# Attention with folded blocks: the own block's scores copied over the preceding block's, two transpositions a unit, and a ring of five buffers for the parted weights

## The chip, the cores and the metric

The kernel runs on one core of a Trainium2 chip. The metric is the device time of one execution in microseconds; the time before is the median of three runs. The profile shows one further execution, recorded by the hardware profiler. Engines are named as in the profile: PE is TensorE's matmul, PEld its weight load, DVE is VectorE, ACT is ScalarE, POOL is GpSimd, SP is SyncE.

## What is computed

Four layers with residual connections over 1040 tokens (16 learned ones ahead of a sequence of 1024), width 1024, in fp32. Layers 0 and 3 are sliding-window attention, layer 1 is an mLSTM, layer 2 an HGRN2. Only the attention is touched (and one small helper in layer 2). Its core, cut to what matters:

```
qb, kb, vb: blocks of 128 tokens; 16 query heads, 4 key heads, width 64
kk = concatenate([prev(kb), kb]); vv = concatenate([prev(vb), vb])
s = einsum('bnqhgd,bnkhd->bnhgqk', qb, kk) * (A_HD ** -0.5)
dist = (arange(BLOCK)[:, None] + BLOCK) - arange(2 * BLOCK)[None, :]
mask = (dist >= 0) & (dist < A_WIN)          # A_WIN = 128 = BLOCK
m = maximum(s.max(axis=-1), sink)
e = exp(where(mask, s, -inf) - m)
p = e / (e.sum(axis=-1) + exp(sink - m))
o = einsum('bnhgqk,bnkhd->bnqhgd', p, vv)
```

A query at place i of its block sees the keys j > i of the preceding block and the keys j <= i of its own: exactly 128 of the 256, one for each j.

## The kernel before, in words

Activations lie transposed (features on partitions, tokens along the free axis) in three chunks of 400, 384 and 256 tokens. Each projection is done with operands parted into a high and a low half of type fp32r: a copy rounds to the high half, a subtraction gives the low half, and three products (high by high, high by low, low by high) replace one. Weights are loaded and parted by `weights` and `split` (copy on ACT, L195, subtraction on DVE, L196); the projections' matmuls are at L231 and L326.

PE's instructions are issued in the order of one long list of steps. Each step is a cost in ns, a function that issues the instructions, and perhaps a function that prepares weights, which is called ahead by a sum of costs (`LOOKAHEAD`). `weave` interleaves two lists in proportion to their costs; `later`, `spread` and `chain` place steps behind others. The orders on DVE, ACT and POOL are left to the framework's planner; `hi` raises a step's priority there. Each engine works off its queue in order.

The attention's core is cut into units: one block of queries, one of the four pairs of query tiles (`ts`, index u) and one half `hh`, so two heads a unit. Layer 0 has 4 x 9 x 2 = 72 units, the last layer, which leaves out block 0, has 64. A unit goes through three steps, and in the list the k-th S step stands behind the T step of unit k - 2 (`T_LAG`) and the V step of unit k - 4 (`V_LAG`), woven with projections.

- `S_step`: scores of two heads against up to 256 keys in one PSUM tile (L726, L727). DVE's tensor_tensor_reduce adds the mask, scales by the query's norm, writes the negated scores to the tile `Sm` and their minimum to `st` (L734). ACT takes the exponential with the sum (L737). POOL, which has put the sinks in the column behind the scores (L731), multiplies by DVE's reciprocal of the sum (L739, L740).
- `T_step`: the weights are transposed into the PSUM tile `pt`, one 128x128 piece for each of two key blocks and two heads, so four (L755). ACT rounds to `Ph` (L757), DVE subtracts for `Pl` (L758).
- `V_step`: value products with `Ph` and `Pl` for each key block (L773); at the end of a group of blocks the result goes out by L781 and L782.

For block 0 there is one key block of 16 tokens, for block 1 one of 16 and one of 128, for the others two of 128. The masks tile holds a 128x128 part for sums over heads and, from column 128, the values 0 inside the band and 1e30 outside it. `Ph`, `Pl` and `Sm` have two buffers each. In layer 0 the second query projection borrows them as temporaries (`idle`).

Of the kernel before, what the change touches and what calls it, by code (L numbers as in the profile page):

```python
# [113 lines left out]
def hybrid_kernel(ctx: ExitStack, tc: tile.TileContext, ins, out, layers=(0, 1, 2, 3)):  # L114
# [29 lines left out]
    def small(w):  # L144
        return tpool.tile([P, w], F32, tag=f"s{w}", name=nm("s"), bufs=12 if w < 8 else 4)

# [333 lines left out]
    def layer_a(i, j, first, last, fin, scale=None):  # L480
# [4 lines left out]
        def enter():  # L485
            R["mix"] = mix = new_mix()
            R["masks"] = masks = mix.tile([P, 384], F32, name=nm("masks"))
            sp.dma_start(masks, ins["a_masks"])
            R["cons"] = cons = mix.tile([P, 18], F32, name=nm("cons"))
            sp.dma_start(cons, ins["a_cols"][j])  # L490
            v.tensor_scalar(cons[:, 0:1], cons[:, 0:1], -0.125, None, op0=ALU.mult)
            v.tensor_scalar(cons[:, 2:18], cons[:, 2:18], -1.0, None, op0=ALU.mult)
# [57 lines left out]
        def idle(n, c0, cn):  # L550
            z = [R["mix"].tile([P, 2, 2, P], F32, tag=z, name=nm(z), bufs=2) for z in ("Ph", "Pl")]
            z = [y.rearrange("p a u q -> p (a u q)") for y in z]
            z.append(R["mix"].tile([P, 2, 257], F32, tag="Sm", name=nm("Sm"), bufs=2).rearrange("p u k -> p (u k)"))
            return [y[:, :cn] for y in z]
# [143 lines left out]
        def mixers():  # L698


            def S_step(w):
# [12 lines left out]
                w["kbs"] = kbs  # L714
                nk = sum(z[2] for z in kbs)
                kw, mo = (nk if b == 0 else 256), {0: 128, 1: 112}.get(b, 0)
                kb = slice(k0, k0 + kw)
                S = psum("pm", 2).rearrange("p (u k) -> p u k", u=2)
                w["Sm"] = Sm = mix.tile([P, 2, 257], F32, tag="Sm", name=nm("Sm"), bufs=2)
                if b == 0:  # L720
# [3 lines left out]
                for u, t in enumerate(w["ts"]):  # L724
# [5 lines left out]
                    if u == 0:  # L730
                        g.tensor_copy(Sm[:nq, :, nk : nk + 1], cons[:nq, 2 + head : 4 + head].rearrange("p (u c) -> p u c", c=1))  # L731
                for u in range(2):
                    rq = R["rq", w["ts"][u], n][:nq, 2 * kq + hh : 2 * kq + hh + 1]
                    v.tensor_tensor_reduce(Sm[:nq, u, :nk], S[:nq, u, :nk], R["masks"][:nq, P + mo : P + mo + nk],  # L734
                                           rq, sinks[u], ALU.add, ALU.min, st[:nq, u : u + 1])
# [7 lines left out]
            def T_step(w):  # L743
                b, kbs, Sm = w["b"], w["kbs"], w["Sm"]
                nq = blk(b)[1]
                kn = NMETA if b == 0 else P
                pt = psum("pt", 1).rearrange("p (k u q) -> p k u q", k=2, u=2)
                w["Ph"] = Ph = R["mix"].tile([P, 2, 2, P], F32R, tag="Ph", name=nm("Ph"), bufs=2)
                w["Pl"] = Pl = R["mix"].tile([P, 2, 2, P], F32R, tag="Pl", name=nm("Pl"), bufs=2)
                if b == 0:  # L750
                    for z in (Ph, Pl):
                        g.memset(z[:, 0, :, :NMETA].bitcast(F32), 0.0)
                for ki, (kb, ko, _) in enumerate(kbs):
                    for u in range(2):
                        pe.transpose(pt[:kn, ki, u, :], Sm[:, u, ko : ko + kn], ident)  # L755
# [386 lines left out]
    def layer_c(i, j, fin):  # L1142
# [3 lines left out]
        def enter():  # L1146
# [9 lines left out]
            def lse(dst, p0, p1):  # L1156
                d = small(8)
                v.tensor_tensor(d, p0, p1, op=ALU.subtract)
# [397 lines left out]
def _layout(inp):  # L1556
# [3 lines left out]
    f["ngain"] = np.asarray(inp["norm_gain"]).reshape(4, KT, P).transpose(2, 0, 1)  # L1560
    am = np.zeros((P, 384), np.float32)
    am[:64, :64] = 1.0
    am[64:, 64:128] = 1.0
    ii = np.arange(P)[:, None]
    jj = np.arange(256)[None]
    am[:, 128:] = np.where((jj > ii) & (jj <= ii + P), 0.0, -BIG)
# [78 lines left out]
```

## Time and profile before

| what | value |
|---|---|
| median of 3 runs | 2595.16 us (2594.36 to 2595.36) |
| profiled execution, its own time | 2594.76 us |
| profiled execution, span from first to last instruction | 2593.0 us |
| mean granted TensorE clock | 0.997 |
| instructions | 54342 |
| POOL busy | 243.4 us |

The span leaves out what lies ahead of the first and behind the last instruction, here 1.8 us. Busy times are the shares in which an engine worked on at least one instruction. Matmuls are pipelined, so the duration of one includes time in which the next runs already; what one matmul costs is read from start to start. The two attention layers lie at about 0 to 460 us and 2140 to 2593 us.

### The profile page before, as it was taken

What the parts mean: (1) busy time and instruction counts of PE and PEld (TensorE: products, weight loads), DVE (VectorE), ACT (ScalarE), POOL (GpSimd) and SP (SyncE); (2) the same over time, 40 slices, a digit from 0 to 9 for tenths busy, and PEclk for the clock granted to TensorE, in tenths of its full rate; (3) what the DMA queues carried; (4) which work ended last, traced back from release to release, by engine and by line L of the source; (5) the groups of instructions that cost most, each with busy time, mean ns of one, the idle gap of its engine ahead of it and who ended that gap; (6) DMA issues with size and microseconds to landing.
All of it is one profiled execution on the core that took longest, in us unless ns stands there. A gap on an engine that the chain in (4) does not pass through costs nothing.

```text
span 2593.0 us, 54342 instructions
## 1 busy us (share of the span) xinstructions
PE 2547.2 (98%) x20446; PEld 2487.2 (96%) x20446; DVE 1949.5 (75%) x5266; ACT 1682.9 (65%) x4403; POOL 243.4 (9%) x564
## 2 busy tenths in 40 slices
PE   8999999999999999999999999999999999999999
PEld 8899999999999999999999999999999999999999
DVE  7897898785657474747475688978878978887996
ACT  8766766576464555555555757877676857767772
POOL 0321231000000000000000000001000000321330
PEclk9999999999999999999999999999999999999999
DMA  5223212021111111111111111111111113212112
GB/s 157 62 66 95 57 43 70 29 67 54 46 50 49 51 41 58 42 50 45 53 42 50 58 35 34 35 35 35 34 42 34 35 51 93 64 43 82 56 42 78
DMA packets 86058, 140.21 MB, mean 54 GB/s; under 512 B 12425, under 2 KB 39186, under 8 KB 85794
## 3 DMA queue, kind: packets, MB, share of 16 engines
q1 hardware_dynamic: 85794, 136.73, 17.1%
q8 instruction: 161, 2.64, 0.4%
q14 instruction: 103, 0.84, 0.1%
HBM read 121.83 MB, written 4.27 MB: 49 GB/s over the span
## 4 chain that ended last, share of the span: by engine, by line
PE 62%; DVE 13%; ACT 8%; issue 2%; DMA 1%; SPq 0%; POOL 0%; DVEq 0%; ACTq 0%; POOLq 0%
PE pj L231 28%; PE pj L326 14%; PE pj L281 10%; DVE wl L196 1%; PE po L1019 1%; PE po L1021 1%; PE pa L1035 1%; ACT X L1269 1%; PE po L773 1%; DVE x L329 1%; PE pj L277 1%; ACT Sm L737 1%; PE pt L755 1%; DVE Sm L734 1%; DVE X L1267 1%
## 5 line engine op out<-in xcount | busy, mean ns | idle before, releaser
L231 PE MATMUL pj<-uh,wh 128*128 128x256 f32 (+2 forms) x2688 | 915.7, 341 | 7.7 <-ACT uh L401 7.2
L231 PE MATMUL pj<-ul,wh 128*128 128x256 f32 (+2 forms) x2688 | 864.3, 322 | 0.3
L231 PE MATMUL pj<-uh,wl 128*128 128x256 f32 (+2 forms) x2688 | 864.6, 322 | 0.0
L231 PEld LDWEIGHTS pj<-uh,wh 128*128 128x128 f32 x2688 | 508.5, 189 | 17.4 <-ACT uh L401 7.2
L231 PEld LDWEIGHTS pj<-ul,wh 128*128 128x128 f32 x2688 | 508.8, 189 | 6.4 <-DVE ul L196 0.8
L231 PEld LDWEIGHTS pj<-uh,wl 128*128 128x128 f32 x2688 | 507.9, 189 | 0.0
L196 DVE TENSOR_TENSOR wl<-wr,wh 128x512 fp32r<-128x512 f32 (+1 forms) x338 | 234.2, 703 | 55.0 <-ACT wh L195 52.1
L195 ACT CAST wh<-wr 128x512 fp32r<-128x512 f32 (+1 forms) x338 | 202.7, 613 | 97.6 <-PE pj L326 31.5
L326 PE MATMUL pj<-yh,wh 128*128 128x384 f32 (+2 forms) x768 | 253.6, 330 | 9.8 <-DVE x L329 8.3
L329 DVE TENSOR_TENSOR x<-x,pj 128x384 f32<-128x384 f32 (+2 forms) x480 | 233.8, 507 | 33.4 <-PE pj L326 32.1
L326 PE MATMUL pj<-yh,wl 128*128 128x384 f32 (+2 forms) x768 | 246.2, 321 | 0.0
L326 PE MATMUL pj<-yl,wh 128*128 128x384 f32 (+2 forms) x768 | 246.2, 321 | 0.0
L281 PE MATMUL pj<-wh,uh 128*128 128x256 f32 (+1 forms) x768 | 232.7, 303 | 0.0
L281 PE MATMUL pj<-wl,uh 128*128 128x256 f32 (+1 forms) x768 | 216.3, 282 | 0.0
L281 PE MATMUL pj<-wh,ul 128*128 128x256 f32 (+1 forms) x768 | 215.9, 281 | 0.0
L737 ACT ACTIVATE Sm<-Sm,s 128x257 f32<-128x257 f32 (+2 forms) x272 | 131.1, 483 | 88.6 <-DVE s L734 86.3
L740 POOL TENSOR_TENSOR Sm<-Sm,s 128x512 f32<-128x512 f32 (+2 forms) x136 | 139.3, 1024 | 406.5 <-DVE s L739 386.3
L458 ACT ACTIVATE t<-t 128x384 f32<-128x384 f32 (+2 forms) x240 | 118.0, 491 | 75.5 <-DVE t L457 74.6
L195 ACT CAST yh<-r 128x384 fp32r<-128x384 f32 (+2 forms) x120 | 57.0, 478 | 156.2 <-PE pj L326 139.4
L326 PEld LDWEIGHTS pj<-yh,wh 128*128 128x128 f32 x768 | 144.9, 189 | 14.0 <-DVE x L329 10.3
L457 DVE SCALAR_TENSOR_TENSOR t<-pj,t 128x400 f32<-128x400 f32 (+2 forms) x168 | 86.3, 513 | 81.5 <-ACT t L456 80.2
L281 PEld LDWEIGHTS pj<-wh,uh 128*128 128x128 f32 x768 | 144.7, 188 | 2.2
(303 smaller groups left out, 5447.1 us busy)
## 6 DMA issues: line engine op xcount, KB each, us to landing
wr<-in_b_win SPq DMA_DIRECT2D x124, 256.0 KB, 2.8
wr<-in_a_win SPq DMA_DIRECT2D x80, 256.0 KB, 2.8
wr<-in_c_win SPq DMA_DIRECT2D x64, 256.0 KB, 3.0
wr<-in_a_wout SPq DMA_DIRECT2D x32, 256.0 KB, 2.8
wr<-in_b_wout SPq DMA_DIRECT2D x32, 256.0 KB, 2.7
t<-t SPq DMA_DIRECT2D x100, 48.0 KB, 1.9
cs<-in_rope SPq DMA_DIRECT2D x11, 400.0 KB, 3.7
cs<-in_rope SPq DMA_DIRECT2D x11, 384.0 KB, 3.5
```

The costliest lines, as they stand in the source:

```text
L195: s.copy(h, src)
L196: v.tensor_tensor(l, src, h.bitcast(F32), op=ALU.subtract)
L231: pe.matmul(acc[:, :cn], a[:, k, :], b[:, k, c0 : c0 + cn], start=(k == 0 and i == 0), stop=(k == KT - 1 and i == 2))
L277: pe.matmul(acc[:48, :nc], um[0][:, k, :], m[:, kk, :], start=(k == 0 and m is wh), stop=(k == KT - 1 and m is wl))
L281: pe.matmul(acc[:cn, :nc], a[:, k, c0 : c0 + cn], m[:, kk, :], start=(k == 0 and j == 0), stop=(k == KT - 1 and j == 2))
L326: pe.matmul(acc[:, :cn], a[:, k, mc], b, start=(k == 0 and i == 0), stop=(k == 1 and i == 2))
L329: v.tensor_tensor(x[:, m, c0 : c0 + cn], x[:, m, c0 : c0 + cn], acc[:, :cn], op=ALU.add)
L457: v.scalar_tensor_tensor(a[:, :cn], z, 0.0, a[:, :cn], op0=ALU.min, op1=ALU.subtract)
L458: s.activation(a[:, :cn], a[:, :cn], AF.Exp)
L734: v.tensor_tensor_reduce(Sm[:nq, u, :nk], S[:nq, u, :nk], R["masks"][:nq, P + mo : P + mo + nk], rq, sinks[u], ALU.add, ALU.min, st[:nq, u ...
L737: s.activation(Sm[:nq, u, : nk + 1], Sm[:nq, u, : nk + 1], AF.Exp, scale=-1.0, bias=st[:nq, u : u + 1], accum_out=den[:nq, u : u + 1])
L740: g.tensor_tensor(Sm[:nq, :, :nk], Sm[:nq, :, :nk], den[:nq].rearrange("p (u c) -> p u c", c=1).to_broadcast([nq, 2, nk]), op=ALU.mult)
```

## The change

For blocks 2 to 8 (b > 1), of a unit's 256 scores only 128 count, one for each place j. The scores of the own block are copied over those of the preceding block where they count (a conditional copy on DVE, inside PSUM, under the mask's bits), and reduction, exponential, normalisation and transposition are done on 128 columns. Behind the two transpositions a minimum with the mask (0 or 1e30) writes the weights out twice, for the preceding and for the own key block, with zeros where the other one counts. ACT rounds this copy to `Ph`, and POOL, no longer DVE, subtracts for `Pl`.

Buffers: `Ph`, `Pl` and the new source tile share a ring of five. `Sm` is 145 columns wide instead of 257. The masks get one column more, so that the mask can be read one column shifted. The small tiles of width 1 have four buffers instead of twelve; width 8 is replaced by a part of a `tmp` tile in layer 2. `idle` takes its three temporaries from the ring of five and from the tag `yl`. The costs in the step list and PE's order are as before.

```diff
     def small(w):
-        return tpool.tile([P, w], F32, tag=f"s{w}", name=nm("s"), bufs=12 if w < 8 else 4)
+        return tpool.tile([P, w], F32, tag=f"s{w}", name=nm("s"), bufs=12 if w == 2 else 4)
...
-            R["masks"] = masks = mix.tile([P, 384], F32, name=nm("masks"))
+            R["masks"] = masks = mix.tile([P, 385], F32, name=nm("masks"))
...
-            z = [R["mix"].tile([P, 2, 2, P], F32, tag=z, name=nm(z), bufs=2) for z in ("Ph", "Pl")]
+            z = [R["mix"].tile([P, 2, 2, P], F32, tag="PP", name=nm(z), bufs=5) for z in ("Ph", "Pl")]
             z = [y.rearrange("p a u q -> p (a u q)") for y in z]
-            z.append(R["mix"].tile([P, 2, 257], F32, tag="Sm", name=nm("Sm"), bufs=2).rearrange("p u k -> p (u k)"))
+            z.append(tpool.tile([P, 400], F32, tag="yl", name=nm("rot"), bufs=YS))
...
-                nk = sum(z[2] for z in kbs)
+                nk = P if b > 1 else sum(z[2] for z in kbs)
...
-                w["Sm"] = Sm = mix.tile([P, 2, 257], F32, tag="Sm", name=nm("Sm"), bufs=2)
+                w["Sm"] = Sm = mix.tile([P, 2, P + NMETA + 1], F32, tag="Sm", name=nm("Sm"), bufs=2)
...
+                if b > 1:
+                    w0 = R["masks"][:, P : 2 * P].bitcast(mybir.dt.uint32).rearrange("p (u k) -> p u k", u=1)
+                    v.copy_predicated(S[:, :, :P], w0.to_broadcast([P, 2, P]), S[:, :, P : 2 * P])
+                    bound = R["masks"][:, 2 * P : 2 * P + 1].to_broadcast([P, P])
+                else:
+                    bound = R["masks"][:nq, P + mo : P + mo + nk]
                 for u in range(2):
                     rq = R["rq", w["ts"][u], n][:nq, 2 * kq + hh : 2 * kq + hh + 1]
-                    v.tensor_tensor_reduce(Sm[:nq, u, :nk], S[:nq, u, :nk], R["masks"][:nq, P + mo : P + mo + nk],
+                    v.tensor_tensor_reduce(Sm[:nq, u, :nk], S[:nq, u, :nk], bound,
                                            rq, sinks[u], ALU.add, ALU.min, st[:nq, u : u + 1])
...
-                pt = psum("pt", 1).rearrange("p (k u q) -> p k u q", k=2, u=2)
-                w["Ph"] = Ph = R["mix"].tile([P, 2, 2, P], F32R, tag="Ph", name=nm("Ph"), bufs=2)
-                w["Pl"] = Pl = R["mix"].tile([P, 2, 2, P], F32R, tag="Pl", name=nm("Pl"), bufs=2)
+                pt = psum("pt", 1)
+                part = lambda z, d: R["mix"].tile([P, 2, 2, P], d, tag="PP", name=nm(z), bufs=5)
+                src = part("Pm", F32) if b > 1 else None
+                w["Ph"], w["Pl"] = Ph, Pl = part("Ph", F32R), part("Pl", F32R)
...
+                if b > 1:
+                    for u in range(2):
+                        pe.transpose(pt[:, P * u : P * u + P], Sm[:, u, :P], ident)
+                    both = pt[:, : 2 * P].rearrange("p (k u q) -> p k u q", k=1, u=2)
+                    keep = R["masks"][:, P + 1 : 3 * P + 1].rearrange("p (k u q) -> p k u q", k=2, u=1)
+                    v.tensor_tensor(src, both.to_broadcast([P, 2, 2, P]), keep.to_broadcast([P, 2, 2, P]), op=ALU.min)
+                    s.copy(Ph, src)
+                    g.tensor_tensor(Pl, src, Ph.bitcast(F32), op=ALU.subtract)
+                    return
+                pt = pt.rearrange("p (k u q) -> p k u q", k=2, u=2)
...
             def lse(dst, p0, p1):
-                d = small(8)
+                d = tmp()[:, :8]
...
-    am = np.zeros((P, 384), np.float32)
+    am = np.zeros((P, 385), np.float32)
...
-    jj = np.arange(256)[None]
+    jj = np.arange(257)[None]
```

## The prediction

> **What bounds the kernel now.** I read the page's busy times first, then the windows view over the stages in which the changed code runs, then PE's waits there. The columns of the windows view are named in its header.
>
> ```profile
> PE 2547.2 (98%) x20446; PEld 2487.2 (96%) x20446; DVE 1949.5 (75%) x5266; ACT 1682.9 (65%) x4403; POOL 243.4 (9%) x564
> ```
>
> ```profile
> core 0: us, PE busy (x) PEld busy (x) DVE busy (x) ACT busy (x) POOL busy (x), PEclk, DMA share, GB/s
> 60.00:460.00 400.00, 386.22 (x2622) 373.95 (x2622) 344.55 (x922) 282.66 (x800) 95.99 (x169) 0.99 0.23 65
> 2140.00:2540.00 400.00, 389.13 (x2666) 380.57 (x2666) 339.26 (x858) 293.01 (x801) 85.26 (x127) 0.99 0.21 63
> 460.00:1540.00 1080.00, 1078.33 (x7177) 1062.18 (x7176) 678.16 (x1700) 607.68 (x1443) 15.23 (x108) 1.00 0.15 48
> ```
>
> ```profile
> PE pt L755 <- POOL Sm L740: 7.4, 7, 2.2
> ```
>
> PE is the bound as a whole. The two attention layers (rows one and two) differ from the rest (row three): PE still idles 13.8 and 10.9 us there, and DVE is busy 86% and 85% of the time instead of 63%. So PE sets the pace with DVE close behind, and what the change is worth depends on both. PE's largest wait in the first attention layer is on the normalised scores, 7.4 us; it ends a chain that goes through DVE's queue.
>
> The same view in 40 us windows shows where DVE leaves almost nothing free:
>
> ```profile
> 100.00:140.00 40.00, 39.92 (x297) 39.29 (x296) 38.03 (x109) 31.67 (x98) 14.75 (x26) 1.00 0.31 87
> 140.00:180.00 40.00, 39.24 (x264) 37.75 (x263) 37.65 (x101) 28.08 (x80) 9.15 (x15) 1.00 0.14 38
> ...
> 300.00:340.00 40.00, 37.99 (x276) 36.90 (x275) 36.86 (x98) 29.18 (x89) 12.75 (x19) 1.00 0.24 64
> ...
> 380.00:420.00 40.00, 37.73 (x253) 37.05 (x252) 37.11 (x90) 32.84 (x85) 11.21 (x16) 0.96 0.25 72
> ...
> 2240.00:2280.00 40.00, 40.00 (x296) 39.69 (x294) 36.76 (x98) 33.57 (x97) 11.78 (x17) 1.00 0.20 57
> 2280.00:2320.00 40.00, 39.73 (x277) 39.02 (x276) 36.31 (x93) 22.45 (x63) 9.93 (x16) 1.00 0.14 47
> ...
> 2440.00:2480.00 40.00, 36.46 (x252) 34.48 (x251) 38.57 (x103) 24.96 (x74) 9.97 (x16) 1.00 0.13 40
> 2480.00:2520.00 40.00, 39.76 (x292) 39.36 (x291) 36.75 (x101) 33.26 (x93) 13.74 (x21) 1.00 0.13 41
> ```
>
> The highest DVE share is 38.57 of 40 us, 96.4%; PE lost 3.5 us in that very window. I take 96.4% as the share at which DVE is full.
>
> **PE: what goes.** A unit is one block of 128 queries for two heads. Layer 0 has 72 units and the last layer 64; 56 in each, 112 in all, have block number 2 or more, and only these change. Each loses two of its four transpositions. What a transposition is worth is read from start to start, since the matmuls overlap:
>
> ```profile
> 253.28 0.35 PE L231 MATMUL pj<-uh,wl 128*128 128x400 f32 x1
> 253.47 0.60 PE L755 MATMUL pt<-ident,Sm 128*128 128x128 f32 x4
> 253.82 0.43 PE L231 MATMUL pj<-uh,wh 128*128 128x400 f32 x1
> 254.09 0.35 PE L231 MATMUL pj<-ul,wh 128*128 128x400 f32 x1
> ```
>
> From the first transposition (253.47) to the second matmul after them (254.09) pass 0.62 us. One 128x400 matmul takes 0.19 us of that, as from 253.28 to 253.47. Four transpositions are thus worth 0.43 us, one 0.109 us. The gain is 224 x 0.109 = 24.4 us, if PE can use it. The score matmuls and the value products stay as they are.
>
> **DVE, ACT, POOL: what each unit pays.** The rows of the groups by shape (mean ns of one stands after the comma):
>
> ```profile
> L734 DVE CUSTOM_DVE_ANT_0 Sm<-pm,masks,cons 128x256 f32<-128x256 f32 x224 | 114.5, 539 | 6.3 <-PE pm L727 5.5
> L734 DVE CUSTOM_DVE_ANT_0 Sm<-pm,masks,cons 128x144 f32<-128x144 f32 x32 | 12.5, 421 | 0.9 <-PE pm L727 0.9
> L758 DVE TENSOR_TENSOR Pl<-pt,Ph 128x512 fp32r<-128x512 f32 x128 | 87.9, 687 | 12.9 <-ACT Ph L757 11.3
> L329 DVE TENSOR_TENSOR x<-x,pj 128x256 f32<-128x256 f32 x160 | 62.9, 415 | 10.4 <-PE pj L326 10.1
> L1004 DVE TENSOR_TENSOR W<-E,pm 128x128 f32<-128x128 f32 x64 | 17.8, 277 | 0.0
> L737 ACT ACTIVATE Sm<-Sm,s 128x257 f32<-128x257 f32 x224 | 113.3, 507 | 73.9 <-DVE s L734 71.8 <-POOL Sm L731 0.7 <-DVE s L739 0.2
> L737 ACT ACTIVATE Sm<-Sm,s 128x145 f32<-128x145 f32 x32 | 13.1, 410 | 9.8 <-DVE s L734 9.7
> L757 ACT CAST Ph<-pt 128x512 fp32r<-128x512 f32 x128 | 74.3, 581 | 13.7 <-PE pt L755 12.7
> L195 ACT CAST wh<-wr 128x512 fp32r<-128x512 f32 x332 | 200.1, 615 | 96.5 <-PE pj L326 30.4 <-DMA wr<-in_b_win 20.3 <-PE pj L231 19.3
> L740 POOL TENSOR_TENSOR Sm<-Sm,s 128x512 f32<-128x512 f32 x112 | 124.2, 1109 | 260.6 <-DVE s L739 242.5 <-DVE rq L603 5.1 <-PE pm L727 4.8
> L740 POOL TENSOR_TENSOR Sm<-Sm,s 128x288 f32<-128x288 f32 x16 | 11.1, 693 | 134.2 <-DVE s L739 132.1 <-PE pt L755 2.0
> ```
>
> - DVE's two masked reductions shrink from 256 to 128 columns. The slope is (539 - 421)/112 = 1.05 ns a column, so each saves 0.135 us and both 0.27.
> - DVE gets the conditional copy, 128x256, from PSUM into PSUM. No row shows it. The nearest is the addition with a PSUM input at L329, as many elements: 0.415 us, which I take. The bounds are half the elements (L1004, 0.277) and twice as many, as if the old contents had to be read too (L758, 0.687).
> - The subtraction leaves DVE and the minimum of the same shape from PSUM takes its place: 0.687 for 0.687, nothing. A broadcast operand could make it a little cheaper or dearer; I know no row that excludes either, and the bounds of the copy cover it.
> - DVE in sum: -0.27 + 0.415 = +0.145 us a unit.
> - ACT: the slope (507 - 410)/112 = 0.87 ns gives 0.11 us less for each of two exponentials; the rounding copy reads SBUF instead of PSUM, 0.615 (L195) for 0.581. In sum -0.19 us on an engine that is 70% busy: worth nothing by itself.
> - POOL: the normalisation falls from 512 to 256 columns; by (1109 - 693)/224 = 1.86 ns a column to 0.63 us. It gains the subtraction of 128x512, for which I take 1.109, the row of its other operation of that size. In sum +0.63 us; its queue has room (row two of the windows, 24%).
> - The five buffers replace two plus two. The unit two before must have finished its value products, as now, so no new wait for a buffer arises. The column added to the masks, the smaller rings of small tiles and the temporary tile in layer 2 cost nothing that I can see; cover: PE's busy 1078 of 1080 us in the middle stage, and at most 1 us if it fails.
>
> **POOL in DVE's way.** One more DVE cost shows in the weight split, whose two inputs both lie in SBUF, first in the middle stage, where POOL hardly works, then in the two attention layers:
>
> ```profile
> L196 DVE TENSOR_TENSOR wl<-wr,wh 128x512 fp32r<-128x512 f32 x154 | 104.0, 687 | 34.7 <-ACT wh L195 33.0 <-PE pa L1094 0.9
> ...
> L196 DVE TENSOR_TENSOR wl<-wr,wh 128x512 fp32r<-128x512 f32 x44 | 33.9, 771 | 2.6 <-ACT wh L195 2.2
> ...
> L196 DVE TENSOR_TENSOR wl<-wr,wh 128x512 fp32r<-128x512 f32 x40 | 29.8, 756 | 0.7 <-ACT wh L195 0.5
> ```
>
> It takes 0.084 and 0.069 us longer beside POOL's work: 44 x 0.084 + 40 x 0.069 = 6.5 us. POOL's normalising and subtracting time grows from 1.109 to 1.74 us a unit, by 57%. For this line alone that adds 3.7 us; for all two-input lines of these stages (rotation, gates, query splits) I estimate twice that, 7.5 us or 0.07 a unit. DVE then pays +0.215 us a unit, 24 us in all.
>
> The Trainium skill (SBUF — State Buffer, Who interferes with whom) says that a DVE instruction with two SBUF inputs contends with a GpSimd instruction that reads SBUF, and that whoever issues first holds the shared ports for its whole instruction. By that rule the new subtraction is in the way and the new minimum and copy are not, since one input is PSUM; the three rows above agree with it, at about 0.08 us on average.
>
> **The sum.** Some 7.5 changed units fall into a 40 us window (112 in about 600 us). PE would need 7.5 x 0.218 = 1.64 us less, 38.36; DVE would need 7.5 x 0.215 = 1.6 us more. Where DVE could be busy to the last moment, the eight windows overflow by what their DVE time exceeds 36.76: 1.27 + 0.89 + 0.10 + 0.35 + 1.81 = 4.4 us. With DVE full at 96.4% (36.98 of 38.36) the limit is 35.38: 2.65 + 2.27 + 1.48 + 1.73 + 1.38 + 0.93 + 3.19 + 1.37 = 15.0 us. I take 11.5, nearer the second: some of DVE's idle time was its wait for ACT's copy ahead of the subtraction (11.3 us in the L758 row), and the minimum doesn't wait for ACT.
>
> Then the new tail of a unit: min on DVE, copy on ACT, subtraction on POOL, one after another. A tight unit of before:
>
> ```profile
> 393.06 0.60 PE L755 MATMUL pt<-ident,Sm 128*128 128x128 f32 x4
> 395.50 0.56 ACT L757 CAST Ph<-pt 128x512 fp32r<-128x512 f32 x1
> 397.20 0.68 DVE L758 TENSOR_TENSOR Pl<-pt,Ph 128x512 fp32r<-128x512 f32 x1
> 399.30 0.28 PE L773 MATMUL po<-Ph,v 128*128 128x256 f32 x1
> ```
>
> The subtraction ends at 397.88, the value products start at 399.30: 1.42 us to spare. The tail grows by 1.109 - 0.687 + 0.615 - 0.581 = 0.46 us, and by 0.63 if a normalisation stands ahead on POOL; 0.3 is left. Behind the subtraction on POOL stand the next unit's sinks and normalisation, for which PE's transpositions wait. I charge 2 us for units that are late.
>
> -24.4 + 11.5 + 2 = -10.9 us from the profiled execution's 2594.8, so 2583.9; the median of the runs is 0.4 higher: **2584**.
>
> The skill's GPSIMD Engine Reference (Elementwise — side-by-side cycle accounting) has a two-input fp32 addition 1.96 times as long on GpSimd as on VectorE; by it the subtraction would be estimated at 1.35 us, 0.24 more than the row's price, which the spare 0.3 us would just take.
>
> **The rivals.**
> - *DVE keeps up*: the work in full windows spills into emptier ones (180 to 220 us has room), and all 24 us are kept: 2571. For it: 14% idle on average. Against it: PE's losses in exactly the windows with DVE above 36.8.
> - *POOL's queue makes the value products late*: POOL works in order, and a subtraction put behind the next unit's normalisation waits until that unit's reciprocal is there.
>
> ```profile
> POOL Sm L740 <- DVE s L739: 386.3, 117, 98.9
> ```
>
> These waits average 3.3 us. If one in eight units (14) is thereby 1 us late or a bit more, some 11 us go on top: 2595, no change. Against it: only the tightest units have under 2 us.
> - *DVE becomes the bound, and it is slower*: the place is the conditional copy, the price 0.687 instead of 0.415, with 0.10 for POOL's interference: DVE pays +0.52 us a unit, 3.9 a window. The limit falls to 33.08, and the eight windows overflow by 4.95 + 4.57 + 3.78 + 4.03 + 3.68 + 3.23 + 5.49 + 3.67 = 33.4 us: -24.4 + 33.4 + 2 = +11, 2606. It decides from where the overflow exceeds 22.4 us, which is 0.93 more a window, 0.12 a unit: a copy above some 0.54 us.
>
> **How the numbers follow.** 0.2% of 2595 is 5.2 us, about what a measurement of this kernel can tell from no change. Forecast 0.42 (2577 to 2590), full gain 0.17 (2569 to 2577), no change by POOL's queue 0.16, slower 0.25 (2600 to 2620). Faster by over 0.2%: 0.58, within 0.17, slower 0.25. The likeliest case's own range is 2577 to 2590; the range over the cases is 2569 to 2610, the upper end short of the copy's and POOL's worst together.
>
> **What would show it.** Right: 288 transpositions instead of 512 of full size; PE's busy time in the stages less by about 24 us; the copy near 0.415 and the reductions near 0.404 us; DVE above 90% in both layers, PE waiting mainly where DVE is over 96%; L196 slower there than 0.77. Wrong: a copy far above 0.54 us; the value products (L773 of before) waiting on POOL often; DVE's share unchanged.

## The result, and the profile after

The changed kernel takes 2600.74 us (median of 8 executions, 2598.13 to 2603.6); the kernel before took 2594.03 us on the same chip. The ratio is 1.0026, with a 95% interval from 1.0015 to 1.0037: 6.7 us slower, where 11 us faster had been forecast. The profiled execution of after took 2598.13 us, its span 2596.3 us.

Below, "us against before" is (ratio - 1) x 2595 us, each ratio against executions of before on the same chip.

The busy times of the page of after:

```profile
PE 2530.8 (97%) x20222; PEld 2462.6 (95%) x20222; DVE 1978.3 (76%) x5378; ACT 1667.6 (64%) x4403; POOL 348.5 (13%) x676
```

The windows view of after, in the columns of before (PE, PEld, DVE, ACT, POOL, granted clock, DMA):

```profile
60.00:460.00 400.00, 375.55 (x2495) 358.75 (x2494) 356.38 (x975) 273.59 (x800) 147.32 (x222) 0.99 0.23 65
460.00:1540.00 1080.00, 1078.25 (x7180) 1061.85 (x7179) 678.51 (x1700) 608.62 (x1443) 15.23 (x108) 1.00 0.15 48
2140.00:2540.00 400.00, 380.19 (x2568) 368.89 (x2567) 355.51 (x921) 283.94 (x800) 136.51 (x183) 1.00 0.22 63
...
140.00:180.00 40.00, 36.77 (x239) 34.70 (x238) 38.63 (x110) 27.80 (x82) 11.75 (x17) 1.00 0.17 49
...
380.00:420.00 40.00, 37.09 (x250) 35.56 (x249) 39.20 (x99) 30.86 (x86) 23.65 (x28) 1.00 0.22 67
...
2440.00:2480.00 40.00, 34.62 (x219) 31.59 (x217) 38.08 (x100) 23.14 (x72) 15.91 (x23) 0.96 0.11 33
```

The middle stage is as it was. In the two attention layers PE has less to do and idles more, 24.5 us of the first 400 instead of 13.8, and DVE's share has risen to 89%. In single 40 us windows DVE works 38 to 39.2 us while PE stands still for 3 to 5. So the freed PE time became waiting. Over the whole kernel PE's waits that DVE ended last rose from 12.7 to 21.5 us, those that POOL ended from 10.0 to 16.7, and ACT's from 18.5 to 22.5.

The groups by shape of after, for the instructions that the change touches:

```profile
L734 DVE COPY_PREDICATED pm<-masks,pm 128x256 f32<-128x256 uint32 x112 | 47.3, 422 | 4.9 <-PE pm L727 3.9
L740 DVE CUSTOM_DVE_ANT_0 Sm<-pm,masks,cons 128x128 f32<-128x128 f32 x224 | 83.7, 406 | 1.7
L765 DVE TENSOR_TENSOR Pm<-pt,masks 128x512 f32<-128x512 f32 x112 | 76.7, 685 | 7.0 <-PE pt L762 4.1 <-POOL Pl L767 1.3 <-POOL Sm L746 0.3
L766 ACT CAST Ph<-Pm 128x512 fp32r<-128x512 f32 x112 | 69.2, 618 | 46.9 <-DVE Pm L765 43.7 <-DVE s L745 2.7
L767 POOL TENSOR_TENSOR Pl<-Pm,Ph 128x512 fp32r<-128x512 f32 x112 | 155.0, 1384 | 105.6 <-ACT Ph L766 95.6 <-ACT rq L606 4.4 <-DMA t<-scaled 3.6
L746 POOL TENSOR_TENSOR Sm<-Sm,s 128x256 f32<-128x256 f32 x112 | 78.9, 705 | 155.0 <-DVE s L745 151.1 <-PE pm L727 2.7 <-ACT Ph L766 1.0
```

The prices on DVE and ACT are those of the forecast to within 0.01 us: the copy 0.422 for 0.415, the reductions 0.406 for 0.404, the minimum 0.685 for 0.687, the rounding copy 0.618 for 0.615. POOL's two are dearer, 1.384 for 1.109 and 0.705 for 0.63. PE's waits on POOL in the whole of after (total us, times, longest):

```profile
PE pt L762 <- POOL Sm L746: 9.9, 14, 1.7
PE pt L772 <- POOL Sm L746: 6.0, 5, 2.2
PE po L790 <- POOL Pl L767: 0.8, 1, 0.8
```

PE waited for a low half once in 112 units. What else changed is in operations that the diff doesn't touch. The last attention layer (2140 to 2540 us) by groups, before:

```profile
L528 DVE TENSOR_TENSOR qs<-t,qs 64x384 fp32r<-64x384 f32 x32 | 18.5, 577 | 3.2 <-ACT qs L527 2.3
L625 DVE TENSOR_TENSOR t<-t,cs 128x384 f32<-128x384 f32 x17 | 10.8, 638 | 2.5 <-DMA t<-t 2.2
L626 DVE TENSOR_TENSOR t<-t,cs 128x384 f32<-128x384 f32 x17 | 10.4, 612 | 0.0
L196 DVE TENSOR_TENSOR wl<-wr,wh 128x512 fp32r<-128x512 f32 x50 | 36.6, 742 | 2.4 <-ACT wh L195 2.2
L329 DVE TENSOR_TENSOR x<-x,pj 128x384 f32<-128x384 f32 x36 | 19.1, 545 | 0.3
```

and after:

```profile
L528 DVE TENSOR_TENSOR qs<-t,qs 64x384 fp32r<-64x384 f32 x32 | 23.4, 731 | 2.6 <-ACT qs L527 1.7
L625 DVE TENSOR_TENSOR t<-t,cs 128x384 f32<-128x384 f32 x17 | 9.5, 559 | 3.0 <-DMA t<-t 2.6
L626 DVE TENSOR_TENSOR t<-t,cs 128x384 f32<-128x384 f32 x17 | 13.1, 770 | 0.1
L196 DVE TENSOR_TENSOR wl<-wr,wh 128x512 fp32r<-128x512 f32 x48 | 35.6, 746 | 2.8 <-ACT wh L195 2.4
L329 DVE TENSOR_TENSOR x<-x,pj 128x384 f32<-128x384 f32 x40 | 21.1, 546 | 0.1
```

The split of the queries (L528) and the rotation's second product (L626) have both inputs in SBUF, and became 27% and 26% longer. The rotation's first product (L625), of the same kind and shape, became shorter (0.638 to 0.559), and the weight split, on which the forecast had based its estimate, hardly moved (0.742 to 0.746). The addition with one input in PSUM (L329) kept its time. So the kind of instruction alone doesn't decide; what runs on POOL beside it does, as experiment 7 shows.

**The theories.** (1) DVE's time: POOL's subtraction reads SBUF while DVE's two-input operations run, these become longer, and DVE is the limit in both layers. (2) POOL's queue: the long subtraction delays the normalisation behind it, or its result comes late. (3) Something beside the core of the change: the helper in layer 2, or the ring of five.

### The profile page after: what moved, and what is told of

Read it like the earlier page. It is cut to its first block, busy times and chain, and to the rows that moved or that the text cites. A ratio compares the mean times of both kernels' runs of the same rounds, so it can differ in the third digit from the quotient of the medians.

```text
span 2596.3 us, 54194 instructions
## 1 busy us (share of the span) xinstructions
PE 2530.8 (97%) x20222; PEld 2462.6 (95%) x20222; DVE 1978.3 (76%) x5378; ACT 1667.6 (64%) x4403; POOL 348.5 (13%) x676
## 5 line engine op out<-in xcount | busy, mean ns | idle before, releaser
L326 PE MATMUL pj<-yh,wh 128*128 128x384 f32 (+2 forms) x768 | 255.0, 332 | 13.5 <-DVE Pm L765 4.5
L329 DVE TENSOR_TENSOR x<-x,pj 128x384 f32<-128x384 f32 (+2 forms) x480 | 234.3, 509 | 32.2 <-PE pj L326 31.2
L767 POOL TENSOR_TENSOR Pl<-Pm,Ph 128x512 fp32r<-128x512 f32 x112 | 155.0, 1384 | 105.6 <-ACT Ph L766 95.6
L326 PEld LDWEIGHTS pj<-yh,wh 128*128 128x128 f32 x768 | 145.5, 190 | 18.5 <-DVE x L329 6.1
L326 PEld LDWEIGHTS pj<-yl,wh 128*128 128x128 f32 x768 | 145.5, 189 | 2.0 <-DVE yl L196 1.6
L281 PEld LDWEIGHTS pj<-wl,uh 128*128 128x128 f32 x768 | 145.5, 189 | 1.9
```

Of the source, the lines that this page charges most:

```text
L281: pe.matmul(acc[:cn, :nc], a[:, k, c0 : c0 + cn], m[:, kk, :], start=(k == 0 and j == 0), stop=(k == KT - 1 and j == 2))
L326: pe.matmul(acc[:, :cn], a[:, k, mc], b, start=(k == 0 and i == 0), stop=(k == 1 and i == 2))
L329: v.tensor_tensor(x[:, m, c0 : c0 + cn], x[:, m, c0 : c0 + cn], acc[:, :cn], op=ALU.add)
L767: g.tensor_tensor(Pl, src, Ph.bitcast(F32), op=ALU.subtract)
```

## The experiments

Diffs are against the changed kernel, except for the second one.

**1. The helper alone (lse_own).**

```diff
-                d = tmp()[:, :8]
+                d = mix.tile([P, 8], F32, tag="lse", name=nm("lse"), bufs=3)
```

> The changed kernel with one part undone: layer 2's small temporary has a tile of its own again, not a part of one of the six tmp tiles. After the change layer 2 starts about 3 us later, relative to layer 1, than before (1500 to 1580 us). If the tmp tile is the cause, this is 3 us faster than the changed kernel, about 2597.5 us, and the shift between 1500 and 1580 us is gone. If that shift comes from the planner's order or by chance, it stays within 1.5 us of the changed kernel, 2600.7.

Measured: 2596.98 us, ratio 1.0007 [0.9999, 1.0016], 1.8 us above before. The 100 us at the start of layer 2 (1500 to 1600), first in after:

```profile
1500.00:1600.00 100.00, 96.73 (x644) 94.97 (x643) 82.82 (x209) 57.79 (x147) 1.16 (x4) 0.98 0.09 28
```

then with a tile of the helper's own:

```profile
1500.00:1600.00 100.00, 98.56 (x668) 97.67 (x667) 83.99 (x212) 60.57 (x151) 1.16 (x4) 1.00 0.10 34
```

PE's time in that stretch comes back (before had 98.56 us too). So taking `d` from the `tmp` ring costs 3.8 us by the medians, 4.9 by the ratios; but the two intervals just touch, and the profiled execution of lse_own, 2599.2 us, is no shorter than that of after, 2598.1, so the size is uncertain. That is part of theory 3. It may be most of the 6.7 us by which after is slower, but it leaves the 11 us of forecast gain missing.

**2. PE's cut alone (pe_alone): before, with two of the four transpositions.**

```diff
-                for ki, (kb, ko, _) in enumerate(kbs):
+                for ki, (kb, ko, _) in enumerate(kbs[:1] if b > 1 else kbs):
...
+                if b > 1:
+                    src = pt[:, :1].to_broadcast([P, 2, 2, P])
```

> The kernel before with two of the four transpositions left out in units of blocks 2 to 8; copy and subtraction read the two that are left twice, so DVE, ACT and POOL do as much as before (the own block's weights are replaced by the preceding block's). It measures what PE can keep of the 24.4 us when nothing else changes. Theory that DVE is full: about half to two thirds, 2578 to 2582 us. Theory that DVE has room and POOL's subtraction eats the gain: all of it, 2570 us.

Measured: 2580.06 us, ratio 0.9944 [0.993, 0.9957], -14.5 us. The windows of the two layers:

```profile
60.00:460.00 400.00, 381.42 (x2558) 366.28 (x2559) 349.11 (x937) 283.26 (x803) 93.47 (x169) 0.99 0.23 65
2140.00:2540.00 400.00, 390.60 (x2608) 381.51 (x2607) 341.14 (x864) 293.56 (x801) 86.90 (x127) 0.98 0.21 62
```

With no work added to DVE, POOL or ACT, 14.5 of the 24.4 us are kept. In the first layer PE idles 18.6 us instead of 13.8.

**3. DVE's copy left out (no_pred), and PE's four transpositions back (four_t).**

```diff
-                    v.copy_predicated(S[:, :, :P], w0.to_broadcast([P, 2, P]), S[:, :, P : 2 * P])
```

```diff
-                    for u in range(2):
-                        pe.transpose(pt[:, P * u : P * u + P], Sm[:, u, :P], ident)
+                    for u in (2, 3, 0, 1):
+                        pe.transpose(pt[:, P * u : P * u + P], Sm[:, u % 2, :P], ident)
```

> The changed kernel without the conditional copy on DVE (the own block's scores are left out of the result). DVE loses 112 x 0.422 = 47 us of work in the two attention layers, all else stays. Theory that DVE is full: 20 to 28 us faster than the changed kernel, 2573 to 2581. Theory that POOL's subtraction holds the units up: at most 6 us faster, 2595 or more.

> The changed kernel with four transpositions again; two of them go into columns that nobody reads. PE gets the 24.4 us back, all else stays. If DVE sets the pace now, PE has room and this costs clearly less than 24 us: 2605 to 2613. If PE still sets the pace, the whole: 2625.

Measured: without the copy 2587.84 us, ratio 0.9974 [0.9964, 0.9983], 13.5 us less than after for 47.3 us of copies; with four transpositions 2608.61 us, ratio 1.0055 [1.0042, 1.0067], 7.5 us more than after for 24.4 us of PE. PE has 17 us of room in the changed kernel. DVE's time counts, though not in full: the 13.5 us lie between what the two theories had let expect. Without the copy another wait appears, the value products' for POOL's low half (0.8 us in after):

```profile
PE po L789 <- POOL Pl L766: 4.2, 6, 1.0
```

**4. The subtraction taken away from POOL: left out, with two buffers a unit instead of three (no_sub), or given to DVE (sub_dve).**

```diff
-                w["Ph"], w["Pl"] = Ph, Pl = part("Ph", F32R), part("Pl", F32R)
+                Ph = part("Ph", F32R)
+                Pl = Ph if b > 1 else part("Pl", F32R)
+                w["Ph"], w["Pl"] = Ph, Pl
...
-                    g.tensor_tensor(Pl, src, Ph.bitcast(F32), op=ALU.subtract)
+                    w["Pl"] = Ph
```

```diff
-                    g.tensor_tensor(Pl, src, Ph.bitcast(F32), op=ALU.subtract)
+                    v.tensor_tensor(Pl, src, Ph.bitcast(F32), op=ALU.subtract)
```

> The changed kernel without POOL's subtraction for blocks 2 to 8: the value products take the high half twice, so the low half is left out of the result. POOL loses 155 us of work, nothing else changes. Theory that POOL's subtraction eats the gain (two-input DVE operations beside it, late value products): 8 us or more faster than the changed kernel, 2592 or less. Theory that DVE's own added work does it: at most 4 us faster, 2597 or more.

> The changed kernel with that subtraction on DVE instead of POOL. DVE gets some 65 to 77 us more, POOL loses 155 us. If DVE is full, 25 us or more slower than the changed kernel, 2625 or more. If POOL's part is the trouble, within 10 us of it, or faster.

Measured: left out 2573.39 us, ratio 0.9926 [0.9914, 0.9939]; on DVE 2622.18 us, ratio 1.0115 [1.0099, 1.013]. The subtraction on POOL costs 26 us, more than the whole gain of PE; on DVE it would cost 49, 23 more than on POOL, a little less than the 25 that the theory of a full DVE had let expect. The busy times without it:

```profile
PE 2523.3 (98%) x20222; PEld 2458.1 (96%) x20222; DVE 1943.8 (76%) x5378; ACT 1666.9 (65%) x4403; POOL 189.8 (7%) x564
```

DVE, which never did this subtraction in after, is rid of 34.5 us when POOL stops doing it, with the same 5378 instructions. That speaks for theory 1, but the ring, POOL's queue and the lateness went too.

**5. Other ways to relieve POOL or DVE (norm_act: normalisation on ACT; rot_pool: the rotation's second product on POOL; both with the helper's own tile).**

```diff
+                if b > 1:
+                    for u in range(2):
+                        s.activation(Sm[:, u, :nk], Sm[:, u, :nk], AF.Identity, scale=den[:, u : u + 1])
+                    return
```

```diff
-                    v.tensor_tensor(rot, rot, cos_sin[:, 1, :cn], op=ALU.mult)
+                    g.tensor_tensor(rot, rot, cos_sin[:, 1, :cn], op=ALU.mult)
```

> The changed kernel with layer 2's temporary in its own tile (2597 us) and, for blocks 2 to 8, the normalisation on ACT (two scaled copies of 128x128) instead of POOL (128x256). POOL loses 79 us of reading beside DVE, ACT gets some 70 us and stays below 80%; DVE's own work is the same. If POOL's interference and its turn in the softmax chain cost something, 4 to 10 us faster than 2597; if only DVE's own work counts, within 2 us of it.

> The changed kernel with layer 2's temporary in its own tile (2597 us) and the rotation's second product on POOL instead of DVE: DVE loses some 31 us in the two attention layers, POOL gets about 55 us. If DVE's own work is what counts, 8 to 15 us faster than 2597; if POOL's work beside DVE costs as much, no gain or slower.

Measured: 2595.44 us, ratio 1.0011 [1.0002, 1.002], and 2600.73 us, ratio 1.0032 [1.002, 1.0045], against 1.0007 [0.9999, 1.0016] for lse_own. 80 us less of POOL's normalising brought nothing measurable. Taken by itself that speaks for DVE's own work, but it doesn't decide: DVE's waits behind POOL, as experiment 7 counts them, fell only from 44.2 us (lse_own) to 39.4, since more of DVE's instructions then ran into the subtraction. More two-operand work on POOL made it slower although DVE's busy total fell from 1976.9 to 1965.8 us; those waits rose to 58.9.

**6. Lateness or not (sub_unused), and POOL held without reading (zero_low, zero_long).**

```diff
                    g.tensor_tensor(Pl, src, Ph.bitcast(F32), op=ALU.subtract)
+                    w["Pl"] = Ph
```

```diff
-                    g.tensor_tensor(Pl, src, Ph.bitcast(F32), op=ALU.subtract)
+                    g.memset(Pl.bitcast(F32), 0.0)
```

> The changed kernel with POOL's subtraction done as it is (1.38 us a unit, from SBUF, behind the same copy), but with the value products taking the high half in place of the low one, so nobody on PE waits for POOL's result (the low half is computed and left out of the sum; the high half counts twice). Without the subtraction the kernel took 2573.4 us, with it 2600.7. If the subtraction costs because the value products get its result late, this gives 2574 to 2580. If it costs because it stands in POOL's queue ahead of the next normalisation, or because it shares SBUF with DVE's two-input operations, this stays at 2596 to 2601 and DVE's busy time stays at about 1978 us. Between 2580 and 2596 both count.

> The changed kernel with POOL's subtraction replaced by POOL writing zeros into the low half (the low half of the weights is left out): the value products still wait for POOL, the ring still hands out three buffers a unit, but POOL reads nothing and needs less time than 1.38 us. If the price is POOL reading SBUF beside DVE or POOL's long hold of its queue, this comes near the kernel without the subtraction: 2573 to 2581, DVE's busy time near 1944 us. If it is the wait of the value products for a further step, or the ring's third buffer, this stays at 2593 to 2601.

Measured: 2599.0 us, ratio 1.0017 [1.0008, 1.0026], and 2574.36 us, ratio 0.9926 [0.9914, 0.9939]. With the subtraction done and nobody waiting for it, 2.3 us come back by the ratios, within the intervals: lateness is not the cause of 26. With zeros written in its place all of it comes back, although the value products wait for POOL and the ring hands out three buffers a unit: neither of these is the cause. Left were the reading and the duration, so zeros were written three times over:

```diff
-                    g.tensor_tensor(Pl, src, Ph.bitcast(F32), op=ALU.subtract)
+                    for _ in range(3):
+                        g.memset(Pl.bitcast(F32), 0.0)
```

> POOL's subtraction replaced by writing zeros into the low half three times over (the low half of the weights is left out). One such writing takes 0.525 us, three take 1.58 us, longer than the subtraction's 1.38 us, and POOL's busy time comes near that of the changed kernel or above it (348 us), but POOL reads nothing. With one writing the time was 2574.4 us. If the subtraction's price is that POOL is held for so long (the next sinks and normalisation stand behind it, and the value products come later), this goes to 2593 to 2601. If it is that POOL reads SBUF beside DVE, this stays at 2573 to 2580, with the weight split on DVE at 0.73 us in the first attention layer instead of 0.78.

Measured: 2573.58 us, ratio 0.9929 [0.9916, 0.9941]. Its busy times:

```profile
PE 2527.6 (98%) x20222; PEld 2461.5 (96%) x20222; DVE 1944.9 (76%) x5378; ACT 1666.8 (65%) x4403; POOL 356.3 (14%) x900
```

and, in the last attention layer, its groups:

```profile
L768 POOL MEMSET Pl<- 128x512 f32 x168 | 88.2, 525 | 6.3 <-ACT Ph L766 0.7
L196 DVE TENSOR_TENSOR wl<-wr,wh 128x512 fp32r<-128x512 f32 x48 | 32.9, 691 | 1.9 <-ACT wh L195 1.7
L528 DVE TENSOR_TENSOR qs<-t,qs 64x384 fp32r<-64x384 f32 x32 | 18.0, 562 | 2.9 <-ACT qs L527 1.9
L626 DVE TENSOR_TENSOR t<-t,cs 128x384 f32<-128x384 f32 x17 | 9.8, 575 | 0.1
```

POOL is busy even longer than in after (356.3 against 348.5 us) and behind it stands the same normalisation, yet the 25 us are gone, and DVE's two-input operations are back at 0.562 and 0.575 us from 0.731 and 0.770. One thing more differs: the zeros don't wait for ACT's rounding, as the subtraction does at the head of POOL's queue (95.6 us). Whether that holds up the normalisation can be read from the traces. The time from the end of DVE's reciprocal to the start of POOL's normalisation, added up over all 136 units, is 15.5 us before, 16.2 in after, 15.4 with the zeros and 13.0 without the subtraction. So POOL's held queue costs at most some 3 us of the 26; its reading is what costs. Theory 2 falls.

**7. How much reading (pool_copy: one copy; copy2: two).**

```diff
-                    g.tensor_tensor(Pl, src, Ph.bitcast(F32), op=ALU.subtract)
+                    g.tensor_copy(Pl, src)
```

> POOL's subtraction replaced by a copy of the masked weights into the low half's place (so the value products add the weights twice; the copy waits for DVE's minimum alone, not for ACT's rounding). POOL reads one operand from SBUF instead of two. If each operand that POOL reads gets in DVE's way, about half of the 26 us should come back: 2582 to 2592, with DVE's busy time near 1960 us. If any reading by POOL holds DVE up for as long as the instruction lasts, this depends on the copy's duration only: near 1.4 us it gives 2598 to 2601, near 0.6 us 2582 to 2588. If POOL's reading is not the price, 2573 to 2580.

> POOL's copy of the masked weights done twice (the value products add the weights twice). Together 1.42 us of POOL reading one operand a unit, as long as the subtraction's 1.38 us with two. With one copy the time was 2578.9 us, with zeros written 2573.6 to 2574.4, with the subtraction 2600.7. If the price goes by the time in which POOL reads at all, this comes near the subtraction: 2594 to 2602, DVE's busy time near 1976 us. If it goes by the second operand, this is the copy's 5 us twice: 2582 to 2587, DVE's busy time near 1960 us.

Measured: 2578.92 us, ratio 0.9949 [0.9935, 0.9963], and 2583.27 us, ratio 0.9966 [0.9953, 0.9978]. POOL's copies in these two kernels:

```profile
L767 POOL CAST Pl<-Pm 128x512 fp32r<-128x512 f32 x112 | 79.6, 711 | 70.0 <-DVE Pm L765 53.6 <-DVE s L745 11.5 <-ACT Sm L743 3.6
```

```profile
L768 POOL CAST Pl<-Pm 128x512 fp32r<-128x512 f32 x224 | 161.2, 720 | 72.7 <-DVE Pm L765 48.7 <-DVE s L745 12.4 <-ACT Sm L743 4.8
```

Two copies are 1.44 us of reading one operand a unit, longer than the subtraction with its two (1.384 us), and cost 10 us over the three writings of zeros, where the subtraction costs 25. So the price does not go by the time in which POOL reads. (One copy alone would not have decided: 2578.92 us lies in the range that its expectation gave to "POOL's reading is not the price".) But two copies differ from the subtraction in two things: they read one operand each, and they are two short instructions instead of a long one. The traces tell which of these matters. A product of the rotation (start and duration in us stand first) beside the subtraction in after:

```profile
2348.72 1.30 POOL L767 TENSOR_TENSOR Pl<-Pm,Ph 128x512 fp32r<-128x512 f32 x1 [1.93 <-ACT Ph L766]
2348.75 1.68 DVE L626 TENSOR_TENSOR t<-t,cs 128x384 f32<-128x384 f32 x1
```

beside two copies in copy2, which stand in one line:

```profile
2411.78 1.49 POOL L768 CAST Pl<-Pm 128x512 fp32r<-128x512 f32 x2
2411.82 0.98 DVE L625 TENSOR_TENSOR t<-t,cs 128x384 f32<-128x384 f32 x1
```

and beside the writing of zeros in zero_long:

```profile
2222.11 1.10 POOL L768 MEMSET Pl<- 128x512 f32 x2
2222.21 0.55 DVE L625 TENSOR_TENSOR t<-t,cs 128x384 f32<-128x384 f32 x1
```

Beside zeros the product takes 0.55 us. Beside the subtraction it took 1.68 and ended at 2350.43, 0.41 us behind the subtraction's end. In copy2 it ended 0.42 us behind the end of the first copy (2412.38) and did not wait for the second. The other way round the subtraction waits: it takes 1.29 us where no DVE instruction with two SBUF inputs runs beside it, and the mean is 1.384. The next table has all DVE instructions with two inputs in SBUF that start while POOL works on the one named; their waiting is what they take above the median of the same shape with POOL at rest.

| kernel | POOL's instruction | alone, us | DVE instructions that start beside it | their waiting, us |
|---|---|---|---|---|
| before | normalising (512 columns in blocks 2 to 8) | 1.04 | 67 | 24.5 |
| after | normalising (256 columns in blocks 2 to 8) | 0.61 | 59 | 11.2 |
| after | subtraction | 1.29 | 57 | 33.9 |
| copy2 | one of two copies | 0.61 | 68 | 13.3 |
| zero_long | one of three writings of zeros | 0.53 | 79 | none |

So each of them waits at most for the end of one instruction of POOL's, 0.59 us on average behind the subtraction and 0.20 behind a copy. The two sums, 33.9 and 13.3 us, differ by the same factor as the prices, 25 and 10 us. So the length of the single instruction that reads explains the price; that a second operand as such costs anything is not shown, because no run has a one-operand instruction of 1.29 us.

**8. The whole computation with single readings (select).** Rounding and subtraction are done on the 128x256 weights before the mask, the subtraction on DVE with one operand in PSUM; POOL then writes each half out twice under a triangular pattern. The helper has its own tile.

```diff
-                    v.tensor_tensor(src, both.to_broadcast([P, 2, 2, P]), keep.to_broadcast([P, 2, 2, P]), op=ALU.min)
-                    s.copy(Ph, src)
-                    g.tensor_tensor(Pl, src, Ph.bitcast(F32), op=ALU.subtract)
+                    high, low = src[:, 0], src[:, 1]
+                    s.copy(high.bitcast(F32R), both[:, 0])
+                    v.tensor_tensor(low.bitcast(F32R), both[:, 0], high, op=ALU.subtract)
+                    for z, y in ((Ph, high), (Pl, low)):
+                        for ki, keep in enumerate((ALU.is_gt, ALU.is_ge)):
+                            g.affine_select(z[:, ki], y, [[0, 2], [2 * ki - 1, P]], keep, 0.0, base=0, channel_multiplier=1 - 2 * ki)
```

> The whole computation, with layer 2's helper in a tile of its own, and with the halves made before the mask: ACT rounds the 128x256 transposed weights to a high half, DVE subtracts for the low half on 128x256 with one operand in PSUM (0.415 us as in other rows, in place of the minimum of 0.685), and POOL writes each half out twice by a select under a triangular pattern, four instructions of 128x256 a unit that read one operand each. If POOL hurts DVE only where it reads two operands, four short single readings cost little (the copy of 128x512 cost 5 us in 112 units) and DVE is rid of 0.27 us a unit, 30 us: 2560 to 2578, faster than both kernels. If any reading by POOL gets in DVE's way for as long as it lasts (four selects of perhaps 0.5 us, 2 us a unit, against the subtraction's 1.38), this gives 2580 to 2600. If the four selects are so long that POOL's queue makes the next unit late, it is above 2600 and PE waits on the normalisation.

Measured: 2568.41 us, ratio 0.9912 [0.9897, 0.9927]: 22.8 us faster than before and 29.5 faster than after, of which the helper's own tile has some 4 to 5. Its busy times:

```profile
PE 2523.0 (98%) x20222; PEld 2462.1 (96%) x20222; DVE 1931.5 (75%) x5378; ACT 1638.4 (64%) x4403; POOL 386.3 (15%) x1012
```

and the groups of its new instructions:

```profile
L769 POOL TENSOR_SCALAR_AFFINE_SELECT Pl<-Pm 128x256 fp32r<-128x256 f32 x224 | 103.8, 484 | 6.8 <-DVE Pm L766 5.4 <-DVE s L745 0.5
L769 POOL TENSOR_SCALAR_AFFINE_SELECT Ph<-Pm 128x256 fp32r<-128x256 f32 x224 | 97.2, 455 | 27.2 <-ACT Pm L765 26.4 <-ACT rq L609 0.2
...
L766 DVE TENSOR_TENSOR Pm<-pt,Pm 128x256 fp32r<-128x256 f32 x112 | 47.1, 420 | 10.2 <-ACT Pm L765 7.7
L765 ACT CAST Pm<-pt 128x256 fp32r<-128x256 f32 x112 | 41.1, 367 | 16.1 <-PE pt L762 12.8 <-POOL Sm L746 1.6 <-POOL Pl L769 0.4
```

POOL works longer than in the changed kernel (386.3 against 348.5 us, 1.79 us a unit of it in four selects), and the kernel is the fastest that was run. A select alone takes 0.41 us, and DVE's instructions waited 11.0 us behind all 448 of them, against 33.9 behind the subtractions. The expectation's condition, that POOL hurts only where it reads two operands, isn't what these waits show; the selects are short. The select version beats both kernels, with the two transpositions that the change was about.

## Where the prediction was wrong, step by step

The measured 2600.7 us lies at the lower edge of the case that the forecast called slower and gave a chance of 0.25; the case that it took, and the direction, failed.

**What bounds the kernel: right in the main.** PE's freed time turned into waiting, and of the 19.6 us by which PE idles more in the two stages, 12.7 lie in the eight windows that were named. DVE isn't full at 96.4%, though: 39.20 of 40 us occurs.

**PE's cut: right in size, not in worth.** PE issues 20222 matmuls instead of 20446, and from start to start a unit's transpositions take 0.22 us in the median instead of 0.44. Taken alone it brings 14.5 of 24.4 us; the overflow working, with nothing added to DVE, would have left 21 (eight windows against 36.98 us: 3.4 us lost). In the select version, where DVE is at 1931.5 us instead of 1949.5, 22.8 us are kept.

**DVE's own instructions: right.** 83.7 - 114.5 + 47.3 + 76.7 - 76.9 = +16.3 us (76.9 is 112 x 0.687 for the subtractions that left), for a forecast of 0.145 x 112 = 16.2. The rival's dear copy didn't come.

**"POOL in DVE's way": the step that failed.** It put the interference "for all two-input lines of these stages" at "7.5 us or 0.07 a unit". Added up over all groups by shape, DVE's operations take 39.2 us more than before; less the 16.3 of its own instructions that is 22.9 us, 0.20 a unit, three times the estimate. (The page's total rises by only 28.8 us because records of neighbouring DVE instructions overlap, and there are 112 more of them.) By the table of experiment 7, DVE's waiting behind POOL's reading rose from 24.5 to 45.1 us, which is 20.6 of these 22.9. That there is such a conflict the prediction had right; two things were wrong in its size. The weight split stood for all lines, and its mean hardly changed: in before 24 weight splits ran beside the normalising, in after 23 beside the subtraction. Of the 46 query splits of 64x384, 17 ran beside the subtraction in after, at 0.914 us instead of 0.566. And POOL's time was taken as one quantity to be scaled by 57%, where it matters what POOL does in it, and in how long a piece: three runs with POOL busy for 346.9 to 356.3 us cost 25 us apart (zeros -18.4, two copies -8.8, subtraction +6.7 us against before).

The Trainium skill (SBUF — State Buffer, Who interferes with whom) has a DVE instruction with two SBUF inputs contend with a GpSimd instruction that reads SBUF, not with one that only writes it. The zeros against the subtraction agree with that, 0.562 against 0.731 us for the same query split. That section of the Trainium skill gives the hold for a whole instruction for DVE's two-port modes, and the prediction took it over for two SBUF inputs; the table of experiment 7 bears that out.

**The price of DVE's time.** The forecast had 24 us on DVE cost 11.5, 0.48 us a us. Across kernels with the same transpositions, the same DVE instruction list but for the subtraction, and only POOL's part of the third step or the subtraction's place changed:

| kernel | DVE busy, us | us against before |
|---|---|---|
| zero_long | 1944.9 | -18.4 |
| pool_copy | 1952.4 | -13.2 |
| copy2 | 1958.4 | -8.8 |
| after | 1978.3 | +6.7 |
| sub_dve | 2012.4 | +29.8 |

From the first to the last that is 48.2 us for 67.5, 0.71 a us, and every row lies within 1.3 us of that line; so do no_sub, zero_low and sub_unused. In sub_dve, the one row where DVE's microseconds come from an instruction of its own, their price is the same as where they come from waiting for POOL. The point at which the forecast's third rival, DVE as the bound, was to become slower than before, 0.215 + 0.12 = 0.335 us a unit, was in fact passed: 39.2/112 = 0.35. With 0.35 the forecast's own working gives a limit of 36.98 - 2.6 = 34.35 us a window, an overflow of 23.2 us, and -24.4 + 23.2 + 2 = +0.8; with 4 for the helper +5, measured +6.7. So the rival came true for another reason than its own: through POOL's reading, not the copy. That the sum comes within 2 us of the measured time is partly luck, since it still holds the 2 us for late units, for which the runs show little.

**POOL's queue and late units: too dear.** The 2 us for late units and the rival of late value products (0.16) have little behind them: one wait of 0.8 us, and nothing measurable came back when nobody waited. "Its queue has room" was right (the 24% are those of the first row of the windows; the second has 21%); that it may be filled with anything was not.

**"At most 1 us" for the helper: wrong.** It is 4 to 5 us by the medians and the ratios, with the uncertainty said in experiment 1. The cover named was the middle stage from 460 to 1540 us, and the loss is in the 100 us after 1500, where layer 2 begins.

**What stays open.** no_pred, rot_pool and select lie off the line of the table. no_pred has DVE at 1947.7 us, which would give about -16 us against before, and measured -6.7; the value products' waits for POOL, 4.2 us instead of 0.8, explain at most 4 of the nearly 10. For rot_pool the line gives -3.5 us, measured +8.3, and for select -28, measured -22.8; what makes up these differences stays open. Nor is it shown whether a second operand costs anything beside the length of the instruction.

## What to carry to other kernels

An idle engine is not free room: ask what its instruction reads, and which operations of the full engine read the same memory at that time. Take the loss from the lines that are likely to collide with it, each by itself, and test it by an instruction of the same length that reads nothing. A mean over a line hides the collisions; look at the single instructions that start beside the new one, and at what their end waits for. Where work must go to POOL, give it short instructions, here 0.41 us instead of 1.29, and keep the steps with two operands on the engine that can take one of them from PSUM.

## What was unexpected of the hardware

- A DVE instruction with two SBUF inputs that starts while POOL reads SBUF waits for the end of POOL's instruction: a product of 0.55 us took 1.68 beside a subtraction of 1.30 us. One that starts first keeps its time, and POOL's instruction gets longer instead: a query split of 0.55 us from 123.67 on in after, and the subtraction from 123.68 on, which took 1.69 us. DVE's instructions with one input in PSUM are not touched (L329 at 0.545 and 0.546).
- A POOL instruction that only writes (zeros, 128x512, 0.525 us) costs its neighbours nothing measurable even three times a unit; a copy that reads one operand for 0.71 us costs 5 us in 112 units, and the subtraction that reads two for 1.384 us costs 25.
- POOL's subtraction of 128x512 took 1.384 us where its normalising product of the same shape had taken 1.109; with no two-input DVE instruction beside them it is 1.29 and 1.04. The longer time is near the 1.35 us that had been worked out from the Trainium skill (GPSIMD Engine Reference, Elementwise — side-by-side cycle accounting).
- A conditional copy of 128x256 inside PSUM takes 0.422 us, as long as an addition of that shape (0.415); a select under a triangular pattern of 128x256 on POOL 0.455 to 0.484 us.
